# Casting and accumulating DMAs for part of the split of streamed weights, in a two-layer encoder trunk on one core

## The chip, the cores and the metric

One core of one Trainium2 chip runs the whole program in one launch. The metric is the device time of an execution in microseconds (us). Engines are called by the profile's names: PE multiplies matrices (PEld is its weight load), DVE, ACT and POOL work element by element, SP issues loads. A DMA is issued by an engine's instruction, runs by itself, and whoever needs its data waits for its landing.

## The reference

Two layers over 512 tokens of width 1024, all in float32: a feed-forward, a token mixer of three parallel attentions, and a second feed-forward; then a last norm.

```python
for l in range(DEPTH):                                   # 2
    x = x + 0.5 * swiglu(rms_norm(x, ffn1_norm[l]), ffn1_w13[l], ffn1_w2[l])   # 1024 -> 2 x 2816 -> 1024
    h = rms_norm(x, mix_norm[l])
    aq, ak, av, bq, bk, bv, cq, ckv, ckr = _split_cols(h @ w_in[l])
    oa, ob, oc = diff_attention(...), window_gqa(...), mla(...)
    proj = jnp.einsum('bsnw,nwd->bsnd', jnp.stack([oa, ob, oc], axis=2), w_branch[l])
    gates = jax.nn.sigmoid(h @ w_gate[l] + b_gate[l]).reshape(b, s_len, N_BRANCH, D_MODEL)
    x = x + jnp.sum(gates * proj, axis=2) @ w_out[l]
    x = x + 0.5 * swiglu(rms_norm(x, ffn2_norm[l]), ffn2_w13[l], ffn2_w2[l])
return rms_norm(x, final_norm)
```

## The kernel before

**Arithmetic.** Activations lie with features down the 128 partitions and the 512 tokens across. A float32 product is made of three products of the type fp32r: each factor is the sum of an upper part (the number rounded to fp32r) and a lower part (the rest), and `mm3` (lines 151 to 157) adds upper x upper (line 155), upper x lower (156) and lower x upper (157). Each is a product of 128x128 weights with 512 columns.

**The stream of weights.** All weights lie in DRAM in the order of their use, as 409 chunks of 128 x 1024 float32 (512 KB), eight blocks of 128x128 each. `Stream` (line 40) hands them out. `load` issues a chunk's load from SP into the tile `wraw` (3 buffers). `_split` (line 63) makes a chunk's parts: ACT copies `wraw` into `whi` (line 71; writing fp32r rounds), DVE subtracts, `wlo = wraw - whi` (line 72). `whi` and `wlo` have 3 buffers each (`WB`), so the parts of chunk c+3 can be written only when PE has done with chunk c. `take` (line 76) gives PE the next block; when it stands at the third block of chunk c, it calls for the split of chunk c+1. Chunk 0 is loaded and split in two pieces (`cuts`).

**Phases.** A feed-forward (`ffn`, line 361) uses 66 chunks: 44 for w13 (tiles `pa`, `pg`), 22 for w2 (tiles `po`). After each of the 8 output tiles of w2 DVE updates x (line 383), and POOL squares it and adds it to a running sum (`square_sum`, lines 254 to 261), for the next norm. The mixer (`mix`, line 740) lays projections (`acc`, `pm`, `pw`) between the steps of the attentions. In `rstd` (263) POOL's power (274) stands between two sets of transposes of PE.

**Order.** Each engine works through its own queue in order. In general the framework chooses the order within a queue by priority and by when it thinks that something is ready; so an instruction can stand ahead of others that were written before it. The start of the program is an exception: in the first feed-forward the order of ACT, DVE and POOL is that of the text, which asks for all eight square sums before the first `take`:

```python
with self.tc.manual_schedule(engines={nc.scalar.engine, nc.vector.engine, nc.gpsimd.engine}):
    for j in range(NT):
        self.next_h(j, None)          # square_sum on POOL
    _, R = self.group_rstd(pss, srcs, h, (6, 8))
```

`group_rstd` takes 48 blocks, which calls for the splits of chunks 0 to 6. Before it, PE multiplies zeros (line 296) eight times while the first loads are under way.

Of the kernel before, what the change touches and what calls it, by code (L numbers as in the profile page):

```python
# [18 lines left out]
T = 512  # L19
# [20 lines left out]
class Stream:  # L40
    """The weights, 128 rows by 128 columns at a time, in the order of their use."""

# [20 lines left out]
    def _split(self, upto):  # L63
        while self.ready < min(upto, self.k.nch):
            c = self.ready
            self.load(c + self.k.AHEAD)
            r = self.raw.pop(c)
            lo = self.k.wp.tile([P, CH], F32R, tag="wlo", bufs=self.k.WB, name="wlo")
            hi = self.k.wp.tile([P, CH], F32R, tag="whi", bufs=self.k.WB, name="whi")
            for part in self.cuts(c):  # L70
                self.k.nc.scalar.copy(hi[:, part], r[:, part])  # L71
                self.k.nc.vector.tensor_tensor(lo[:, part], r[:, part], hi[:, part].bitcast(F32), ALU.subtract)  # L72
            self.split[c] = (hi, lo)
            self.ready += 1
# [12 lines left out]
    def fit(self, width):  # L87
        """Fills a chunk that has no room for so wide a block."""
        while self.pos % CH + width > CH:
            self.order.append((None, P))  # L90
            self.pos += P


class Kernel:
    RAW, AHEAD, WB = 3, 2, 3  # chunks of weights: buffers as loaded, loads ahead, buffers of their parts
    UNITS, PTS = 72, 4  # tiles of 512 and of 1024 columns
    WARM = 8  # products of zeros that raise TensorE's clock while the first loads are under way
    LAG = 1  # steps between the scores of a block of queries and the rest
    FILL0, RATES = (0, 1), (0.35, 0.6, 0.85)  # how much other work goes between an attention's steps

# [11 lines left out]

    # ---- tiles
    def u(self, dt=F32, shape=(P, T), name="u"):
# [26 lines left out]

    # ---- pieces
    def lookup(self, *args, **kw):
        """An activation that needs a table of its own; these keep their order, so that tables change seldom."""
        if self.last is None:
            self.last = self.nc.scalar.activation(*args, **kw)
        else:
            with self.tc.issue_after(self.last.ins):
                self.last = self.nc.scalar.activation(*args, **kw)

    def mm3(self, ps, w, x, start, stop):
        """ps += w^T x, each float32 as the sum of two parts that one pass carries."""
        (wh, wl), (xh, xl) = w, x
        mm = self.nc.tensor.matmul
        mm(ps, wh, xh, start=start, stop=False)  # L155
        mm(ps, wh, xl, start=False, stop=False)  # L156
        mm(ps, wl, xh, start=False, stop=stop)  # L157

    def proj(self, ps, src, xs):
        """128 output features for all tokens; src(k) names a block of weights."""  # L160
        n = len(xs)
        for k in range(n):
            self.mm3(ps, self.w.take(src(k)), xs[k], k == 0, k == n - 1)
# [15 lines left out]
    def group(self, pss, srcs, xs):  # L179
        """Several projections side by side, so that the last of xs is needed late. With no xs,  # L180
        they are made on the way from x."""
        n = len(xs) or NT
        for k in range(n):
            for ps, src in zip(pss, srcs):
                while len(xs) < min(k + (1 if ps is pss[0] else 3), n):
                    xs.append(self.gsplit(self.x[len(xs)], self.g(0, G_FFN1, len(xs)), "h"))
                self.mm3(ps, self.w.take(src(k)), xs[k], k == 0, k == n - 1)
            yield

    def group_rstd(self, pss, srcs, xs, at=(4, 6)):  # L190
        """A group, with the scale of the tokens worked out meanwhile."""
        res = g = None
        for k, _ in enumerate(self.group(pss, srcs, xs), 1):
            if k in at:
                g = g or self.rstd(self.sqacc, D, self.att)
                try:
                    next(g)
                except StopIteration as e:
                    res = e.value
        return res  # L200
# [4 lines left out]
    def stacked(self, src, name):  # L205
        """The parts of two heads' rows, each head's one above the other: the first head's with the
        upper part on top, the second's with the lower one."""
        out = []
        for m in range(2):
            t = self.u(F32R, name=name)  # L210
            own, other = slice(m * 64, m * 64 + 64), slice(64 - m * 64, 128 - m * 64)
            self.nc.scalar.copy(t[own], src[own])
            self.nc.vector.tensor_tensor(t[other], src[own], t[own].bitcast(F32), ALU.subtract)
            out.append(t)
        return out

    def doubled(self, src, name):
        """Of two heads' rows, each head's upper part twice above each other, and the lower parts."""
        out = []
# [12 lines left out]
    def mm_stacked(self, ps, q, m, c, kh, kl, start, stop):  # L232
        """ps += q^T k over 64 rows: q as stacked, the upper part of k twice above each other."""
        own = slice(m * 64, m * 64 + 64)
        self.nc.tensor.matmul(ps, q[:, c], kh, start=start, stop=False)
        self.nc.tensor.matmul(ps, q[own, c], kl[own], start=False, stop=stop)
# [10 lines left out]
    def gsplit(self, src, g, name="g"):  # L247
        """The parts of src times a gain per partition."""
        hi, lo = self.pair(name)
        self.nc.scalar.activation(hi, src, AF.Copy, scale=g)  # L250
        self.nc.vector.scalar_tensor_tensor(lo, src, g, hi.bitcast(F32), ALU.mult, ALU.subtract)  # L251
        return hi, lo
# [10 lines left out]
    def rstd(self, acc, dim, bank, evac=True):  # L263
        """From sums of squares: 1/rms per token, down the partitions and across them. Yields
        where TensorE would wait."""
        nc = self.nc
# [17 lines left out]

    # ---- set-up
    def setup(self):
# [48 lines left out]

    # ---- feed-forward
    def next_h(self, j, gcol):
        """x's tile j is final: its part of the next norm's input."""
        h = None if gcol is None else self.gsplit(self.x[j], gcol, "h")
# [71 lines left out]

    # ---- the three mixers
    def scaled(self, ps, R, by=None):
# [7 lines left out]
    def rproj(self, src, xs, R, by=None):  # L421
        """A projection of normalised tokens: the scale of a token comes after the product."""
        ps = self.acc()
# [6 lines left out]
    def vproj(self, xs, src, out, banks):  # L430
        """Values with tokens down the partitions, 512 features wide."""
        pss = [b("pv") for b in banks]
# [25 lines left out]
    def flip(self, p, n, hi, lo):  # L458
        """The parts of p's transposed blocks; hi and lo take n blocks side by side."""
        ps = self.att("tp")  # L460
# [4 lines left out]
    def pv(self, ps, v, pth, ptl):  # L465
        """ps += values^T probabilities^T over four blocks of keys, for two blocks of queries."""
        mm = self.nc.tensor.matmul
# [7 lines left out]
    def full_pv(self, hd, qb, d, v, st):  # L475
        """Transposes the probabilities of a block of queries; after two blocks, their products with the values."""
        if qb == 0:
# [12 lines left out]
    def heads(self, n, steps, prepare, first, second):  # L490
        """All heads' steps in one line: scores of a step, then the rest of the step before; the
        next head's projections in between. Yields where other work may go."""
        todo = []
# [81 lines left out]
    def vproj_b(self, l, h, R, v):  # L575
        """Values of both key heads, each head's parts side by side."""
        t = yield from self.win(l, [(2176, P)], h, R)
# [16 lines left out]
    def branch_b(self, l, v, kk, h, R, qs, out):  # L594
# [42 lines left out]
        def second(j, hf, ps):  # L637
# [5 lines left out]
            for m in range(2):  # L643
# [6 lines left out]
                yield  # L650
                # above, the upper parts of the values; below, the lower ones
                side = slice(m * 256, m * 256 + 256)
# [87 lines left out]
    def mix(self, l):  # L740
# [26 lines left out]
        z2, z0, z1 = [], [], []  # L767
        # compressed projections of C
        cols = [[(2688 + i * P, P)] for i in range(2)] + [[(2944, 64), (2976, 32), (2944, 32)]] + [[(2304 + i * P, P)] for i in range(3)]
# [103 lines left out]
def gather(order, nch, inp):  # L873
    """The weights' blocks, in the order of their use."""
    out = np.zeros((P, nch * CH), np.float32)
    at = 0
# [85 lines left out]
```

## Time and profile before

| | us |
|---|---|
| median of 2 runs (2548.07 to 2548.37) | 2548.22 |
| span of the profiled execution | 2544.7 |
| PE busy in it | 2524.1 |
| DVE busy | 1355.1 |
| ACT busy | 936.2 |
| POOL busy | 270.6 |

The span runs from the first to the last instruction of the profiled execution; the runs are 3.5 us above it. A product's row shows 0.39 us, but products are pipelined: the next one starts 0.23 us later, and that is the pace. A row of the timeline gives start, duration, engine, line, operation, what it writes and reads, and in square brackets how long the engine was idle before it and what ended that.

### The profile page before, as it was taken

To read this page: it belongs to the slowest core of one execution; us is meant where nothing else is said; L and a number is where in the kernel's file an instruction comes from. 1 tells how busy PE (TensorE), PEld (TensorE's weight loads), DVE (VectorE), ACT (ScalarE), POOL (GpSimd) and SP (SyncE) were. 2 spreads that over 40 slices of the span, in tenths; PEclk is the share of its full clock that TensorE was granted. 3 is DMA by queue.
4 is the path that set the end of the run, shared out by engine and by line. 5 is a ranking of instruction groups with operands and counts; after the bars stand their busy time and mean duration, and the time that the engine had idled before them with its cause. 6 is when DMAs were issued, how large, how long until landed. Compare 5 with 4: busy or idle time off the path is not lost.

```text
span 2544.7 us, 28509 instructions
## 1 busy us (share of the span) xinstructions
PE 2524.1 (99%) x11424; PEld 2044.0 (80%) x11424; DVE 1355.1 (53%) x2004; ACT 936.2 (37%) x1429; POOL 270.6 (11%) x208
## 2 busy tenths in 40 slices
PE   9999999999999999999999999999999999999997
PEld 7888887777777888888888888877777788888886
DVE  6444336666667554443344443366666676544433
ACT  4332223365555433332233322244655553322211
POOL 4000123000001220001100001130000014100011
PEclk9999999999999999999999999999999999999999
DMA  4333332112212233333333333321222122333331
GB/s 159 93 97 100 95 122 86 59 58 75 67 58 67 88 94 100 93 97 100 95 96 100 93 98 99 106 81 51 67 75 66 56 70 89 102 97 94 100 99 67
DMA packets 62484, 223.22 MB, mean 88 GB/s; under 512 B 7200, under 2 KB 7344, under 8 KB 62352
## 3 DMA queue, kind: packets, MB, share of 16 engines
q1 hardware_dynamic: 60912, 217.67, 27.6%
q0 software_dynamic: 864, 2.70, 0.3%
q8 instruction: 89, 1.46, 0.2%
q10 hardware_dynamic: 576, 1.05, 0.1%
q14 instruction: 43, 0.35, 0.0%
HBM read 219.29 MB, written 2.10 MB: 87 GB/s over the span
## 4 chain that ended last, share of the span: by engine, by line
PE 95%; DVE 3%; ACT 1%; issue 1%; POOL 0%; DMA 0%; SPq 0%; DVEq 0%; POOLq 0%; ACTq 0%
PE pa L157 7%; PE pa L155 7%; PE pa L156 7%; PE acc L155 7%; PE po L155 6%; PE po L157 6%; PE po L156 6%; PE acc L156 6%; PE acc L157 6%; PE pg L156 5%; PE pg L155 5%; PE pg L157 5%; PE tp L462 2%; PE pm L155 2%; PE pm L157 2%; PE pm L156 2%
## 5 line engine op out<-in xcount | busy, mean ns | idle before, releaser
L72 DVE TENSOR_TENSOR wlo<-wraw,whi 128x1024 fp32r<-128x1024 f32 (+1 forms) x410 | 526.8, 1285 | 641.9 <-ACT whi L71 640.7
L71 ACT CAST whi<-wraw 128x1024 fp32r<-128x1024 f32 (+1 forms) x410 | 429.7, 1049 | 820.0 <-PE po L156 254.4
L155 PE MATMUL pa<-hh,whi 128*128 128x512 f32 x800 | 312.6, 391 | 0.9 <-DVE x L851 0.9
L157 PE MATMUL pa<-hh,wlo 128*128 128x512 f32 x800 | 311.7, 390 | 1.0 <-DVE wlo L72 1.0
L156 PE MATMUL pa<-hl,whi 128*128 128x512 f32 x800 | 311.7, 390 | 0.0
L155 PE MATMUL acc<-hh,whi 128*128 128x512 f32 x672 | 275.4, 410 | 0.0
L156 PE MATMUL acc<-hl,whi 128*128 128x512 f32 x672 | 263.9, 393 | 0.0
L157 PE MATMUL acc<-hh,wlo 128*128 128x512 f32 x672 | 263.5, 392 | 0.0
L155 PE MATMUL pg<-hh,whi 128*128 128x512 f32 x608 | 236.5, 389 | 0.0
L156 PE MATMUL pg<-hl,whi 128*128 128x512 f32 x608 | 236.5, 389 | 0.0
L157 PE MATMUL pg<-hh,wlo 128*128 128x512 f32 x608 | 236.5, 389 | 0.0
L155 PE MATMUL po<-ah,whi 128*128 128x512 f32 x576 | 224.1, 389 | 0.0
L156 PE MATMUL po<-al,whi 128*128 128x512 f32 x576 | 224.1, 389 | 0.0
L157 PE MATMUL po<-ah,wlo 128*128 128x512 f32 x576 | 224.1, 389 | 0.0
L155 PEld LDWEIGHTS pa<-hh,whi 128*128 128x128 f32 x800 | 150.4, 188 | 33.2 <-DVE x L851 1.3
L157 PEld LDWEIGHTS pa<-hh,wlo 128*128 128x128 f32 x800 | 150.3, 188 | 33.1 <-DVE wlo L72 1.9
L156 PEld LDWEIGHTS pa<-hl,whi 128*128 128x128 f32 x800 | 150.3, 188 | 31.2 <-DVE hl L251 0.3
L155 PEld LDWEIGHTS acc<-hh,whi 128*128 128x128 f32 x672 | 126.3, 188 | 32.5 <-issue 9.0
L157 PEld LDWEIGHTS acc<-hh,wlo 128*128 128x128 f32 x672 | 126.2, 188 | 27.7 <-issue 0.2
L156 PEld LDWEIGHTS acc<-hl,whi 128*128 128x128 f32 x672 | 126.6, 188 | 22.3 <-issue 0.9
L155 PEld LDWEIGHTS pg<-hh,whi 128*128 128x128 f32 x608 | 114.2, 188 | 23.8
L157 PEld LDWEIGHTS pg<-hh,wlo 128*128 128x128 f32 x608 | 114.1, 188 | 23.7
(248 smaller groups left out, 3906.5 us busy)
## 6 DMA issues: line engine op xcount, KB each, us to landing
wraw<-in_w SPq DMA_DIRECT2D x408, 512.0 KB, 3.5
x<-in_x SPq DMA_DIRECT2D x8, 256.0 KB, 6.4
rope<-in_rope POOLq DMA_DIRECT2D x6, 256.0 KB, 3.7
out<-o ACTq DMA_DIRECT2D x4, 256.0 KB, 2.9
out<-o SPq DMA_DIRECT2D x4, 256.0 KB, 3.4
dist<-in_cst POOLq DMA_DIRECT2D x1, 448.0 KB, 4.0
wraw<-in_w SPq DMA_DIRECT2D x1, 384.0 KB, 4.6
lv<-in_lam POOLq DMA_DIRECT2D x1, 256.0 KB, 3.9
```

The costliest lines, as they stand in the source:

```text
L71: self.k.nc.scalar.copy(hi[:, part], r[:, part])
L72: self.k.nc.vector.tensor_tensor(lo[:, part], r[:, part], hi[:, part].bitcast(F32), ALU.subtract)
L155: mm(ps, wh, xh, start=start, stop=False)
L156: mm(ps, wh, xl, start=False, stop=False)
L157: mm(ps, wl, xh, start=False, stop=stop)
L462: self.nc.tensor.transpose(ps[:, i * P:(i + 1) * P], p[:, i * P:(i + 1) * P], self.ident)
```

## The change

Of four chunks (counted c % 4) two are split in another way; loads, buffers and order of the rest stay as written.

- c % 4 == 1: `whi` isn't copied by ACT. POOL issues a DMA from DRAM that reads the chunk a second time and converts it to fp32r. DVE still subtracts.
- c % 4 == 3: ACT copies `whi` as before. Then ACT writes `wlo = -wraw` (rounded to fp32r), and POOL issues a DMA that adds `wraw` to `wlo`. DVE doesn't subtract.

```diff
             hi = self.k.wp.tile([P, CH], F32R, tag="whi", bufs=self.k.WB, name="whi")
+            nc = self.k.nc
             for part in self.cuts(c):
-                self.k.nc.scalar.copy(hi[:, part], r[:, part])
-                self.k.nc.vector.tensor_tensor(lo[:, part], r[:, part], hi[:, part].bitcast(F32), ALU.subtract)
+                if c % 4 == 1:
+                    nc.gpsimd.dma_start(hi[:, part], self.k.ws[c][:, part])
+                else:
+                    nc.scalar.copy(hi[:, part], r[:, part])
+                if c % 4 == 3:
+                    nc.scalar.mul(lo[:, part], r[:, part], -1.0)
+                    nc.gpsimd.dma_start(lo[:, part], r[:, part], accum_op=ALU.add)
+                else:
+                    nc.vector.tensor_tensor(lo[:, part], r[:, part], hi[:, part].bitcast(F32), ALU.subtract)
```

Besides, comments and docstrings are gone.

## Rows read from the trace of the kernel before

**Rows 1.** The page: busy time of the engines; PE's granted clock in 40 slices.
```profile
PE 2524.1 (99%) x11424; PEld 2044.0 (80%) x11424; DVE 1355.1 (53%) x2004; ACT 936.2 (37%) x1429; POOL 270.6 (11%) x208
PEclk9999999999999999999999999999999999999999
```

**Rows 2.** Waits of PE: for whom, us in total, times, longest.
```profile
PE pr L278 <- POOL r L274: 3.6, 3, 2.1
PE st L269 <- DVE sqacc L392: 2.2, 1, 2.2
PE pa L157 <- DVE wlo L72: 1.0, 2, 0.7
```

**Rows 3.** The page's groups: the two instructions of the split.
```profile
L72 DVE TENSOR_TENSOR wlo<-wraw,whi 128x1024 fp32r<-128x1024 f32 (+1 forms) x410 | 526.8, 1285 | 641.9 <-ACT whi L71 640.7
L71 ACT CAST whi<-wraw 128x1024 fp32r<-128x1024 f32 (+1 forms) x410 | 429.7, 1049 | 820.0 <-PE po L156 254.4
```

**Rows 4.** Timeline in w13 of the first feed-forward: a split, its first user.
```profile
101.44 1.05 ACT L71 CAST whi<-wraw 128x1024 fp32r<-128x1024 f32 x1 [3.11 <-PE pa L156]
102.53 1.23 DVE L72 TENSOR_TENSOR wlo<-wraw,whi 128x1024 fp32r<-128x1024 f32 x1 [0.21 <-ACT whi L71]
112.30 0.39 PE L155 MATMUL pg<-hh,whi 128*128 128x512 f32 x1
112.32 1.05 ACT L71 CAST whi<-wraw 128x1024 fp32r<-128x1024 f32 x1 [3.11 <-PE pa L156]
112.76 0.39 PE L157 MATMUL pg<-hh,wlo 128*128 128x512 f32 x1
```

**Rows 5.** DMA queue of the weights, and issues: KB each, us to landing.
```profile
q1 hardware_dynamic: 60912, 217.67, 27.6%
wraw<-in_w SPq DMA_DIRECT2D x408, 512.0 KB, 3.5
rope<-in_rope POOLq DMA_DIRECT2D x6, 256.0 KB, 3.7
dist<-in_cst POOLq DMA_DIRECT2D x1, 448.0 KB, 4.0
DMA to landing us min/median/max: 3.1/3.5/7.2
```

**Rows 6.** Timeline of POOL at the start.
```profile
9.56 1.62 POOL L261 TENSOR_TENSOR sqacc<-sqacc,sq 128x512 f32<-128x512 f32 x1
11.15 1.49 POOL L260 TENSOR_TENSOR sq<-x 128x512 f32<-128x512 f32 x1
...
31.11 1.28 POOL L261 TENSOR_TENSOR sqacc<-sqacc,sq 128x512 f32<-128x512 f32 x1
```

**Rows 7.** Timeline of DVE and PE at the start.
```profile
11.66 2.06 DVE L72 TENSOR_TENSOR wlo<-wraw,whi 128x1024 fp32r<-128x1024 f32 x1
1.49 3.78 PE L296 MATMUL idle<-idle 128*128 128x512 f32 x8 [1.49 <-DVE idle L293]
12.42 0.39 PE L155 MATMUL pa<-hh,whi 128*128 128x512 f32 x1
13.77 0.50 PE L157 MATMUL pa<-hh,wlo 128*128 128x512 f32 x1 [0.74 <-DVE wlo L72]
```

**Rows 8.** POOL's square sums: durations in ns, min/median/max.
```profile
L260 POOL TENSOR_TENSOR sq<-x x48: 1039/1042/2023, 7.8 to 2515.0; 128x512 f32<-128x512 f32 x48
L261 POOL TENSOR_TENSOR sqacc<-sqacc,sq x48: 1282/1618/2155, 9.6 to 2516.2; 128x512 f32<-128x512 f32 x48
```

**Rows 9.** Stretches: us, busy time by engine, PEclk, DMA share, GB/s.
```profile
560.00:850.00 290.00, 289.56 (x1376) 226.33 (x1376) 193.44 (x404) 155.30 (x306) 20.77 (x18) 1.00 0.22 69
2530.00:2544.00 14.00, 1.77 (x8) 1.13 (x8) 5.63 (x10) 1.10 (x2) 3.52 (x3) 0.59 0.40 150
```

**Rows 10.** Timeline in the mixer: the split that comes latest, its user.
```profile
551.52 1.99 ACT L71 CAST whi<-wraw 128x1024 fp32r<-128x1024 f32 x2
561.18 0.39 PE L155 MATMUL acc<-hh,whi 128*128 128x512 f32 x1
```

## The prediction, made before the changed kernel ran

> **What bounds the kernel now.** I read the page first: PE is busy for 99% of the span and its clock is granted in full throughout [rows 1]. Next, the waits of PE: the three largest are 3.6, 2.2 and 1.0 us in the whole run, and only the last is for weights [rows 2]. So time is the number of products times 0.23 us, and no relief of another engine can give back more than about 10 us. The change can only leave PE fed, or starve it. What decides is how early a chunk's parts are ready.
>
> That is read from the timeline in w13 [rows 4]. A chunk there feeds PE for 24 products, 5.44 us. ACT's copy at 101.44 waited for PE's last product with the buffer's old content, and starts as soon as that ends. Two more chunks lie in between: the next copy, at 112.32, starts with PE's first product of the next chunk but one, and the first user of the chunk copied at 101.44 is the product at 112.30; its lower part is first read at 112.76. From the release of the buffer a chunk has thus 10.9 us to get its upper part, 11.3 us to get the lower one. Copy and subtraction use 2.3 us of it (102.53 + 1.23 = 103.76). So 8 to 9 us are spare, chunk after chunk. Four feed-forwards of 66 chunks go like this, 264 of 409. In the mixer a chunk takes longer, as attention's products lie between: 72 chunks in some 540 us, 7.5 us each.
>
> **What the change removes.** Chunks 0 to 408 hold 102 of each changed kind. DVE loses 102 subtractions of 1.285 us [rows 3], 131 us. ACT loses 102 copies and gains 102 negations of the same size, both about 1.05 us [rows 3]: nothing. Neither engine sets the end [rows 2], so I cost the relief at 0; what hides it is PE's own queue of products.
>
> **The casting DMA in the steady stages.** No DMA of before converts. POOL's plain loads land 3.7 us (256 KB) and 4.0 us (448 KB) after their issue [rows 5]; by that slope 512 KB take 4.1 us. The weights' own loads from SP land in 3.5 us, at most 7.2 us [rows 5]. Lower bound 3.5, upper 7.2; I take 4.1, the row of the same queue. With DVE's subtraction behind it (1.29 us) the lower part is there 5.4 us after the release, at most 8.5 us, of 11.3: hidden. DVE's queue stands at that subtraction until the DMA lands, some 3 us longer than it stood for ACT, and evacuations of PSUM stand behind it. In w13 the next of those is due one chunk (5.44 us) later; in the mixer DVE is busy for 193 of 290 us [rows 9] and softmax steps stand behind it, with PE having projections to do meanwhile. I put 4 us on this for the whole run, an estimate between 0 and the 10 us that all waits of PE amount to now.
>
> **The accumulating DMA in the steady stages.** It waits for copy and negation: 2 x 1.05 = 2.1 us. Then it reads `wraw` and the old `wlo` and writes `wlo`. The queue of the weights shows what a plain 512 KB cost in transfer: 27.6% of 2544.7 us for 217.67 MB [rows 5], that is 702 us for 415 pieces, 1.7 us each. Lower bound of the landing 3.5 us, as a plain load; with a second reading 4.1 + 1.7 = 5.8 us, which I take, being an estimate from the nearest rows; upper 7.2 + 1.7 = 8.9 us. The lower part is ready at 2.1 + 5.8 = 7.9 us, at most 11.0 us, of 11.3. Hidden, but by 0.3 us only at the far end. PE would begin to wait when the DMA needs more than 11.3 - 2.1 = 9.2 us. The tightest place in the mixer is chunk 91 (91 % 4 = 3, counted along line 71): the second of the two copies at 551.52 ends at 553.5, and its first user is the product at 561.18 [rows 10]; 553.5 + 1.05 + 5.8 = 560.4, just in time.
>
> `wraw` is held longer, until the DMA has read it, so the load of chunk c+3 is issued about 8 us after the release instead of 2.3. It lands by about 12, and is wanted by a copy 16.3 us (three chunks) after the release: hidden. The DMA engines go from 28% to at most 28 + 7 (casting) + 14 (accumulating, twice) = 49%.
>
> **The start.** Here POOL's queue decides. The order is written by hand: eight square sums, then the splits. Chunk 1 is the first with c % 4 == 1, so its upper part, made by ACT at 9.71 before, now comes from a DMA that POOL can issue only behind all square sums, which end at 31.11 + 1.28 = 32.4 us [rows 6]. PE wants that part at 12.42 [rows 7]. All other blocks add to the same sums behind it; PE stands.
>
> How long? DVE stops at its subtraction of chunk 1 (before at 11.66 [rows 7]), waiting for the same DMA, and no longer slows POOL: a pair of square and sum goes from up to 2.02 + 2.16 down to 1.04 + 1.28 us [rows 8], 2.44 us with the gaps. Six pairs are left at 11.15 [rows 6]: they end at 11.15 + 14.6 = 25.8 us. DMA 4.1 us: 29.9. Subtraction 1.29 us and a tenth: 31.3. The product that read this lower part at 13.77 [rows 7] so comes 17.5 us later. Bounds: 25.8 + 3.5 + 1.3 - 13.8 = 16.8 us below; 32.4 + 7.2 + 2.1 - 13.8 = 27.9 us above. I take 17.5, since DVE certainly stops. By the Trainium skill (DMA: Bandwidth & Descriptors, section "Anatomy of one DMA"), a DMA issued from GpSimd takes 2.0 us plus its bytes at 436 GB/s, an estimate of 3.2 us for 512 KB; the rows say 4.1, and by the page this term would be 16.6.
>
> PE idles some 17 us in this. The profile shows what that does to its clock: behind the last products, in 2530 to 2544 with PE busy for 1.8 us, the granted clock is 0.59 [rows 9], and at the start the first eight products (of zeros) took 3.78 us, 0.47 each instead of 0.23 [rows 7]. If eight to ten products go at half pace after the stall, that is 2 us. Range 0 to 3.
>
> Chunk 3's accumulation stands behind chunk 1's DMA on POOL, but is issued at about 27 us for a need beyond 42; chunk 5's cast waits for chunk 2's buffer. Both are hidden by PE's own delay. POOL's power for the first norm comes behind them and is not wanted before block 48.
>
> **Sum.** 17.5 + 2 + 4 = 23.5 us. The profiled execution's 2544.7 becomes 2568; the runs lie 3.5 us above it, 2548.2 becomes about 2572.
>
> **Rivals.**
> (1) The accumulating DMA is slow. From 9.2 us on, each of the 66 of the feed-forwards costs PE the excess: at 11 us 66 x 1.8 = 119 us, hence 2690; the whole passes 2% (51 us, what a measurement of this kernel can tell from no change) at 9.2 + 27.5 / 66 = 9.6 us. Against it: the upper bound by rows is 8.9. For it: nothing in the trace accumulates. What would push it over is a mechanism like this: POOL's writing of a DMA's orders waits out instructions of DVE; one subtraction of 1.29 us before each would make it 5.8 + 1.3 = 7.1, two 8.4, three 9.7. The Trainium skill (SBUF — State Buffer, sections "SBUF: two separate sides" and "Who interferes with whom") has that rule for DVE's two-port modes and not for two-input instructions like this subtraction; by it, an estimate, the steady chunks of w13 lose nothing. No row of before shows such a DMA under DVE's load. Chance 0.14.
> (2) POOL's order in the steady stages. A DMA can stand behind a square sum that itself waits for x. If the framework leaves DMAs where they are written, at a chunk's third block, 6 blocks or 4.1 us ahead of need, a cast lands 4.1 + 1.3 us later, and behind a square sum some 3 us later still. Of 22 chunks of w2 11 are changed; if 4 in each of four feed-forwards stand so, 16 x 3 = 48 us: 2620. Against it: ACT's copies are written at the same place and yet go at the release [rows 4], so such instructions are moved ahead. Chance 0.06.
> (3) The start costs nothing, because the DMA of chunk 1, which waits for nothing, is put ahead of the square sums despite the order by hand: 2548 + 4 = 2552. ACT and DVE keep the text's order there, so I give it 0.09.
> (4) Faster by 2%: only if DVE, 131 us lighter, was what held PE. Waits of PE of 10 us in all exclude it: 0.01.
>
> **How the numbers follow.** Forecast as summed, 0.70, its own range 2560 to 2590 (start from 16.8 to 27.9, clock 0 to 3, steady 0 to 10): 2572. Rivals (3) 0.09, (2) 0.06, (1) 0.14. The range for 8 in 10 takes in the forecast and part of (3) and (2): 2552 to 2620. Slower by over 2% (above 2599): (1), (2) and a rest, 0.20. Faster 0.01. Within 2%: 0.79.
>
> **What would show it.** In the changed profile: PE idle from about 13 to 31 us, its waits naming `whi` or `wlo` of chunk 1, and POOL's first casting DMA right behind the last sum at about 26 us. In w13, landings of accumulations under 9 us, and no waits of PE for `wlo`. DVE's busy time down by 131 us, ACT's unchanged. Wrong I am if PE's waits name `wlo` in every fourth chunk (rival 1), if they gather in w2 (rival 2), or if PE is busy at 20 us (rival 3).

## The result, and the profile after

The changed kernel takes 2579.16 us (2577.81 and 2580.52) against 2548.22: 1.0121 times as long, 95% interval 1.0102 to 1.0141. That is 31 us more. The forecast was 2572 in a range of 2552 to 2620. The profiled execution has a span of 2576.0 us, 31.3 above that of before.

The page of the changed kernel, engines, granted clock, POOL's DMA queue and the two new kinds of DMA (KB each, us to landing):

```profile
PE 2528.4 (98%) x11424; PEld 2043.9 (79%) x11424; DVE 1230.2 (48%) x1902; ACT 930.1 (36%) x1429; POOL 408.1 (16%) x412
...
PEclk8999999999999999999999999999999999999998
...
q1 hardware_dynamic: 60912, 217.67, 26.3%
q0 software_dynamic: 30240, 109.67, 18.5%
...
whi<-in_w POOLq DMA_DIRECT2D x102, 512.0 KB, 3.9
wlo<-wraw POOLq DMA_DIRECT2D x102, 512.0 KB, 4.6
```

DVE is 125 us lighter than in [rows 1], ACT 6 us. PE has the same 11424 products and is busy for only 4 us more: what is lost is idle PE. The waits of PE (us in total, times, longest) against [rows 2]:

```profile
PE pa L163 <- DMA whi<-in_w: 17.2, 1, 17.2
PE pr L286 <- POOL r L282: 6.1, 6, 2.1
PE st L277 <- DVE sqacc L400: 2.2, 1, 2.2
PE cs L710 <- ACT kch L248: 2.1, 2, 1.3
PE acc L163 <- DVE vl L259: 2.0, 1, 2.0
PE po L480 <- DVE ptl L249: 2.0, 2, 1.5
```

One wait of 17.2 us names a casting DMA. The rest is small and scattered, and names POOL, DVE and ACT, not the new DMAs. Lines have moved: 163 to 165 are `mm3` (before 155 to 157), 73 the casting DMA, 75 ACT's copy, 77 its negation, 78 the accumulating DMA, 80 DVE's subtraction, 282 POOL's power.

**Where the 31.3 us are.** The n-th product of PE after, set beside the n-th before, tells how far PE is behind. The order of products differs only inside the mixers (345 of 11424 have other names), so the shift is read at the borders of stages. Each row is one profiled execution against the one of before.

| kernel (below) | shift at 60 us | behind mixer 1 | behind mixer 2 | span |
|---|---|---|---|---|
| changed | 19.2 | 23.2 | 28.8 | +31.3 |
| start as before | 1.7 | 5.9 | 13.2 | +15.9 |
| chunk 1's cast first | 15.2 | 19.3 | 27.2 | +30.1 |
| feed-forwards only | 1.8 | 1.3 | 1.3 | +1.3 |
| chunk 1 only | 19.2 | 19.3 | 19.2 | +19.4 |
| mixers only | 0.4 | 3.8 | 10.0 | +10.9 |
| mixers, casts only | 1.7 | 7.0 | 13.0 | +13.1 |
| mixers, accumulations only | 1.4 | 0.4 | 0.6 | +0.6 |
| mixers, copy after | 1.8 | 1.8 | 1.9 | +2.4 |
| without the costly places | 1.9 | 0.3 | 0.5 | +0.5 |

In the four kernels of the table whose names begin with "mixers" the start is that of before, and still it comes out 0.4 to 1.8 us later. The execution of before that was profiled is one of the shorter ones: its span is 2544.7 us, and other executions of the same kernel have 2543.9 to 2547.6. So shifts under 2 us at the start say nothing. For the changed kernel the table reads: start 19, first mixer 4.1, second mixer 5.6, the four feed-forwards 0 to a tenth, and 2.5 us behind the last product. By medians of several executions the start alone costs 17 to 18 us (runs "chunk 1 only" and "start as before").

**The start**, timelines of POOL, DVE and PE of the changed kernel:

```profile
24.26 1.26 POOL L269 TENSOR_TENSOR sqacc<-sqacc,sq 128x512 f32<-128x512 f32 x1
25.46 0.58 POOL L73 DMA_DIRECT2D whi<-in_w  x1
26.04 0.93 POOL L78 DMA_DIRECT2D wlo<-wraw  x1
...
29.58 1.22 DVE L80 TENSOR_TENSOR wlo<-wraw,whi 128x1024 fp32r<-128x1024 f32 x1 [18.00 <-DMA whi<-in_w]
...
29.60 0.79 PE L163 MATMUL pa<-hh,whi 128*128 128x512 f32 x1 [17.18 <-DMA whi<-in_w]
```

The casting DMA is issued right behind the last square sum, at 25.46 us; before, that sum ended at 32.4 with DVE at work beside it [rows 6]. PE, which had its product at 12.42 [rows 7], has it at 29.60. Its first twelve products then go at a slower pace, one every 0.43 to 0.67 us instead of 0.23, and the shift grows from 17.2 to 19.1 us. In the 5.6 us from 29.60 on, which they fill, the granted clock is 0.50, the lower of its two levels, 1.2 of 2.4 GHz; from 35.3 on it is 1.00. The stretch from 30 to 60 us (columns as in [rows 9]) has a granted clock of 0.91 where it was 1.00 before:

```profile
30.00:60.00 30.00, 29.96 (x123) 24.03 (x123) 9.72 (x12) 4.74 (x5) 3.45 (x3) 0.91 0.48 142
```

**The steady stages.** A stretch of 140 us in w13 of the first feed-forward:

```profile
95.00:235.00 140.00, 140.00 (x619) 115.95 (x618) 55.42 (x70) 42.48 (x53) 9.39 (x13) 1.00 0.52 145
```

The landings of the casting DMAs, then of the accumulating ones, over the whole run:

```profile
DMA to landing us min/median/max: 3.7/3.9/5.6
...
DMA to landing us min/median/max: 4.5/4.6/6.0
```

PE is busy for all of it. A casting DMA needs at most 5.6 us, with a subtraction of 1.3 us behind it, and the lower part had 11.3 us [rows 4]. An accumulating one needs at most 6.0 us, and there was room for 9.2.

**The second mixer**, DVE and PE of the changed kernel:

```profile
1709.31 1.66 DVE L80 TENSOR_TENSOR wlo<-wraw,whi 128x1024 fp32r<-128x1024 f32 x1 [5.23 <-DMA whi<-in_w]
1710.89 2.71 DVE L259 SCALAR_TENSOR_TENSOR vl<-pv,r,vh 128x512 fp32r<-128x512 f32 x4
...
1711.68 0.50 PE L163 MATMUL acc<-hh,whi 128*128 128x512 f32 x1 [2.03 <-DVE vl L259]
```

DVE stands for 5.23 us at a subtraction whose upper part hasn't landed. Behind it in DVE's queue are four instructions that empty PSUM tiles, and PE waits 2.03 us for one of them. The chunk itself isn't wanted yet. From 1702 to 1713 us PE's shift grows from 23.2 to 26.6: 3.4 of the 5.6 us of this mixer. Beside the 2.03 us PE waits 0.9 and 1.4 us there for POOL's two powers; before, its waits for POOL came to 1.1 us in the whole mixer.

That the part comes so late has a reason in POOL's queue. ACT's copy of this chunk (281) and POOL's first power, in the kernel before:

```profile
1677.20 1.05 ACT L71 CAST whi<-wraw 128x1024 fp32r<-128x1024 f32 x1 [2.73 <-issue]
1679.28 1.02 POOL L274 TENSOR_TENSOR r<-ms,mhalf 128x4 f32<-128x4 f32 x1 [3.77 <-DVE ms L272]
```

POOL's power and the casting DMA, in the changed kernel:

```profile
1703.35 1.03 POOL L282 TENSOR_TENSOR r<-ms,mhalf 128x4 f32<-128x4 f32 x1 [3.64 <-DVE ms L280]
1704.72 0.63 POOL L73 DMA_DIRECT2D whi<-in_w  x1 [0.34 <-issue]
```

PE was 23.2 us behind then, so ACT's copy would have stood at 1700.4, and the buffer was free by that time. The DMA is issued 4.3 us later, because it stands behind a power that waits 3.64 us for DVE. Issued at 1700.4 it would have held DVE for about 1 us instead of 5.23, an estimate from the 4.6 us to its landing. Of the 36 casts of the mixers 31 are issued at most 1 us later than ACT's copies of before, moved by PE's shift; of the other five this one is the latest.

### The profile page after: what moved, and what is told of

Read it like the earlier page. It is cut to its first block, busy times and chain, and to the rows that moved or that the text cites. A ratio compares the mean times of both kernels' runs of the same rounds, so it can differ in the third digit from the quotient of the medians.

```text
span 2576.0 us, 28842 instructions
## 1 busy us (share of the span) xinstructions
PE 2528.4 (98%) x11424; PEld 2043.9 (79%) x11424; DVE 1230.2 (48%) x1902; ACT 930.1 (36%) x1429; POOL 408.1 (16%) x412
## 5 line engine op out<-in xcount | busy, mean ns | idle before, releaser
L80 DVE TENSOR_TENSOR wlo<-wraw,whi 128x1024 fp32r<-128x1024 f32 (+1 forms) x308 | 391.4, 1273 | 577.0 <-ACT whi L75 301.4
L75 ACT CAST whi<-wraw 128x1024 fp32r<-128x1024 f32 (+1 forms) x308 | 322.5, 1047 | 701.5 <-PE po L164 270.2
L163 PE MATMUL pa<-hh,whi 128*128 128x512 f32 x800 | 313.5, 392 | 18.1 <-DMA whi<-in_w 17.2
L78 POOL DMA_DIRECT2D wlo<-wraw x102 | 90.3, 885 | 1023.3 <-ACT wlo L77 665.3
L73 POOL DMA_DIRECT2D whi<-in_w x102 | 57.8, 567 | 684.6 <-PE pa L165 177.0
```

The costliest lines, as they stand in the source:

```text
L73: nc.gpsimd.dma_start(hi[:, part], self.k.ws[c][:, part])
L78: nc.gpsimd.dma_start(lo[:, part], r[:, part], accum_op=ALU.add)
```

## The experiments

All times but one (accumulate three times) are medians of several executions beside several of the kernel before; the ratios are to those. Where the trace tells more finely than the times, the table above is quoted.

**Start as before.** Chunks 1 and 3 split as in the kernel before.

```diff
-                if c % 4 == 1:
+                if c % 4 == 1 and c > 4:
-                if c % 4 == 3:
+                if c % 4 == 3 and c > 4:
```

> Chunks 1 and 3 are split as in the kernel before, all other chunks as in the changed one. Theory (the start's stall is additive): the changed kernel's first 60 us lose 19.1 us (17.2 of PE's wait for chunk 1's upper part, 1.9 of slow products after it). They go, but chunk 5's casting DMA now is the first behind the square sums: they end at about 32.4, it lands at 36.5, DVE's lower part is there at 37.7, and PE wants it at 36.1: 1.6 us. 2579.2 - 19.1 + 1.6 = 2561.7; range 2559 to 2564. Rival (the DMAs' general load costs PE time wherever it runs, the start is only where it shows first): the rest of the run takes up part of what the start gives back, 2568 or more.

Measured: 2560.96 us, 1.0052 (1.0037 to 1.0067). 18 us of the 31 are gone, and the rest of the run doesn't take them up. The mixers cost 4.2 and 7.4 us here. The 1.6 us for chunk 5 can't be told from the spread of the start, and no wait of PE there names a casting DMA.

**Chunk 1's cast first.** The casting DMA of chunk 1 is written ahead of the square sums, nothing else moves. (Not shown: the split of chunk 1 takes this tile and issues no DMA of its own.)

```diff
+                self.w.first = self.wp.tile([P, CH], F32R, tag="whi", bufs=self.WB, name="whi")
+                nc.gpsimd.dma_start(self.w.first, self.ws[1])
                 for j in range(NT):
                     self.next_h(j, None)
```

> As the changed kernel, but the casting DMA of chunk 1 is written ahead of the eight square sums. Theory (the place in POOL's queue is what costs): PE no longer waits for chunk 1, but chunk 3's accumulating DMA is still behind the square sums. Those end at about 32.5 with DVE at work beside them; 0.9 + 4.6 us later it has landed, 37.5, and PE wants the lower part at 24.8: a new stall of 12.7 us, and about 1 of slow products. 2548.2 + 13.7 + 9.7 (mixers) + 2.5 (end) = 2574; range 2571 to 2578. Rival A (chunk 1's DMA is late by itself, whatever its place): stays at 2579. Rival B (only the cast counts, the accumulation is hidden): 2560.

Measured: 2576.1 us, 1.0111 (1.0096 to 1.0126). PE's longest wait:

```profile
PE pa L166 <- DMA wlo<-wraw: 11.0, 1, 11.0
```

The stall for chunk 1 is gone and chunk 3's accumulation, still behind the sums, has taken its place: shift at 60 us 15.2 instead of 19.2. Rivals A and B fall. It is the place in POOL's queue that costs: chunk 1's DMA behind the sums, and with that one out of the way chunk 3's. A DMA for which PE has more time there, as chunk 5's in the run above, costs nothing that can be told from the spread.

**Chunk 1 only.**

```diff
-                if c % 4 == 1:
+                if c == 1:
-                if c % 4 == 3:
+                if False:
```

> Only chunk 1 gets its upper part by a casting DMA, everything else is as in the kernel before. Theory: the whole start's loss with nothing else, 2548.2 + 19.1 = 2567.3, and no longer closing drain, as POOL's queue held one DMA more only; range 2566 to 2569. Rival (the stall is shared with chunk 3's accumulation, or the lateness is caught up later because ACT and DVE get ahead during it): under 2562.

Measured: 2564.89 us, 1.0069 (1.0054 to 1.0084), 17 us more than before and 1 us under the range expected. One DMA of 409 chunks makes more than half of the whole loss. The shift is 19.2 at 60 us and 19.2 at the end: PE catches nothing up, since it had no idle time to catch up with.

**Feed-forwards only.** Both conditions get `and c > 4 and not (66 <= c < 138 or 270 <= c < 342)`.

> DMAs only for chunks of the feed-forwards from chunk 5 on; chunks 1 and 3 and those of both mixers (66 to 137, 270 to 341) are split as before. Theory (hidden in the feed-forwards, all remaining cost sits in the mixers and at the end): 2548.2 + 1.6 (chunk 5) + 2.5 (closing drain of POOL) = 2552.3; range 2549 to 2554. Rival (66 casts and 66 accumulations of the feed-forwards cost a tenth each): 2562 or more.

Measured: 2547.69 us, 1.000 (0.9991 to 1.001). 65 casts and 65 accumulations (those of the feed-forwards less chunks 1 and 3) cost nothing. The 2.5 us expected at the end didn't come either.

**Mixers only**, the complement: both conditions get `and (66 <= c < 138 or 270 <= c < 342)`.

> DMAs only for the chunks of the two mixers (66 to 137, 270 to 341), everything else split as in the kernel before: the complement of the run with feed-forwards only. Theory: all that the changed kernel loses beside its start sits here, 11.5 us by the run with the start as before (4.1 and 7.4 us in the two mixers), and up to 2.5 us in POOL's closing drain: 2547.7 + 11.5 = 2559.2, with the drain 2561.7; range 2556 to 2562. Rival (the loss needs DMAs in the feed-forwards as well, whose traffic makes the mixers' loads late): under 2553.

Measured: 2558.65 us, 1.004 (1.0025 to 1.0055): 10 us, with a shift of 3.3 and 6.2 us over the two mixers. The loss needs no DMAs elsewhere.

**Mixers, casts only; mixers, accumulations only.** Of the two conditions of the kernel above one is made `False`.

> Only the casting DMAs, only in the mixers. Theory A (DVE stands at its subtraction until the cast has landed, with evacuations behind it that PE waits for, and POOL's power stands behind the DMA's issue): most of the 11.5 us, 7 or more: 2555 to 2560. Theory B (the accumulations carry the loss, by the longer issue of 0.9 us on POOL and the later landing): 3 us or less, under 2551.

> Only the accumulating DMAs, only in the mixers. Theory A: nothing on DVE waits for them, only POOL's queue is longer: 4 us or less, 2548 to 2552. Theory B (the accumulations carry the loss): 7 us or more, 2555 to 2560.

Measured: casts 2559.44 us, 1.0043 (1.0026 to 1.006); accumulations 2547.39 us, 0.9996 (0.9987 to 1.0005). The casts carry all of it. 36 accumulations, with the longer issue (0.88 us against 0.56) and the later landing, cost nothing. Theory B falls. DVE's wait for casts in the kernel with casts only, and in its timeline the place that answers to the one shown above:

```profile
DVE wlo L80 <- DMA whi<-in_w: 46.0, 19, 8.1
```

```profile
1693.31 1.23 DVE L80 TENSOR_TENSOR wlo<-wraw,whi 128x1024 fp32r<-128x1024 f32 x1 [4.35 <-DMA whi<-in_w]
1694.45 2.72 DVE L259 SCALAR_TENSOR_TENSOR vl<-pv,r,vh 128x512 fp32r<-128x512 f32 x4
```

**Mixers, idle cast (inconclusive).** To take DVE's wait away and keep POOL's queue, ACT copies as before and the cast goes into a tile that nobody reads. There are no accumulations here or in the next run (those lines of the edit are left out).

```diff
+                if c % 4 == 1 and (66 <= c < 138 or 270 <= c < 342):
+                    nc.gpsimd.dma_start(self.k.scratch, self.k.ws[c][:, 0:512])
```

> As the run with casts in the mixers only, but each casting DMA there writes a tile that nobody reads (the first 512 of the chunk's 1024 columns, so half the bytes), and ACT copies the upper part as in the kernel before. DVE waits for no DMA; POOL's queue holds the same issues. Theory (two causes side by side: DVE standing at its subtraction until the landing, and POOL's power or square sums standing behind a DMA's issue that waits): only the second is left, by PE's waits for POOL some 4 us: 2550 to 2555. Rival A (POOL's queue is all of it): 2558 or more. Rival B (DVE's standing is all of it): 2549 or less.

Measured: 2585.01 us, 1.0145 (1.0128 to 1.0161). Nothing in the program read what these DMAs wrote, and the framework moved all 36 to the front: they run from 2 to 139 us, ahead of and between the square sums. The shift is 38 us at 60 us and doesn't grow afterwards. It says nothing of the mixers, and once more that the start is where POOL's queue costs PE.

**Mixers, copy after.** The same with a tie: the DMA reads the upper part that ACT has just made, so it can't leave its place.

```diff
             self.split[c] = (hi, lo)
+            if c % 4 == 1 and (66 <= c < 138 or 270 <= c < 342):
+                nc.gpsimd.dma_start(self.k.scratch, hi[:, 0:512].bitcast(F32))
```

> Casts in the mixers only, in number and place on POOL as in the run with casts there, but each is issued after ACT has made the upper part as in the kernel before, reads that (half of its columns) and writes a tile that nobody reads. So DVE waits for no DMA, while POOL's queue keeps the issues at nearly the same places among its other work. Theory (two causes: DVE standing at its subtraction until a cast has landed; POOL's powers and sums standing behind a DMA's issue): the second alone is left, by PE's waits for POOL in the run with casts (5.7 us in the mixers against 1.4 before) some 4 us: 2550 to 2555. Rival A (POOL's queue is all of it): 2558 or more. Rival B (DVE's standing is all of it, directly or by what queues behind it): 2549 or less.

Measured: 2548.08 us, 1.000 (0.9991 to 1.001). No loss. POOL's queue at the place that cost most, with the DMA between the two powers just as in the kernel with casts:

```profile
1681.12 1.04 POOL L284 TENSOR_TENSOR r<-ms,mhalf 128x4 f32<-128x4 f32 x1 [3.77 <-DVE ms L282]
1682.13 0.62 POOL L82 DMA_DIRECT2D scratch<-whi  x1
1682.93 1.03 POOL L284 TENSOR_TENSOR r<-ms,mhalf 128x4 f32<-128x4 f32 x1 [0.18 <-DVE ms L282]
```

The theory of two causes falls, rival B stands: what stands behind the new DMAs in POOL's queue costs nothing in the mixers. PE's waits for POOL's power go back to the 3.6 us of [rows 2], though the DMA still stands between the two powers; so in the kernel with casts they depend on DVE's being late. What the kernel with casts has and this one hasn't is DVE waiting for a DMA. (Its DMAs also read DRAM, twice the bytes, and land later, 3.9 us against 2.3. No wait of PE there names a cast, and the weights' loads land in 3.6 us in both, so that this reaches PE by another way is not seen; no run excludes it by itself.)

One thing this run can't show: what the casts themselves lose by what stands in front of them on POOL. Nobody reads its DMAs, so their being late holds up no one. For chunk 281 the timelines above show that loss, 4.3 us, and in the kernel with casts the same place looks alike (issue at 1689.25, behind a power at 1688.24 that waited 3.76 us for DVE). A run that issues this one cast ahead of the power was not made.

**Accumulate three times.** Each accumulation from chunk 5 on is followed by two more that add zeros; the sum is unchanged.

```diff
                     nc.gpsimd.dma_start(lo[:, part], r[:, part], accum_op=ALU.add)
+                    if c > 4:
+                        for _ in range(2):
+                            nc.gpsimd.dma_start(lo.rearrange("p (a b) -> p a b", a=2), self.k.zero[:, None, :].broadcast_to([P, 2, 512]), accum_op=ALU.add)
```

> As the changed kernel, but from chunk 5 on each accumulation is followed by two more into the same tile that add zeros, each waiting for the one before. Theory (a chunk's lower part has 11.3 us from the release of its buffer, and 9.2 us of that for DMAs): 2.1 + 3 x 4.7 = 16.2 us, so PE waits 4.9 us for the lower part of every fourth chunk of the feed-forwards, 65 times, 319 us, and a part of the mixers' 36 as well: 2579 + 320 + 0 to 60, 2890 to 2960. Its waits name the lower part. Rival (there is more room than that, because the framework's order gives the chunk a longer lead when the DMA is known to be long): under 2700.

Measured: 3626.54 us, one execution. Far more than expected, and the reason is in the added DMAs, not in the room. One chunk, ACT's copy and negation, POOL's three DMAs, PE's first product with the lower part (timeline):

```profile
155.94 1.05 ACT L75 CAST whi<-wraw 128x1024 fp32r<-128x1024 f32 x1 [1.98 <-PE pa L167]
...
158.24 0.86 POOL L78 DMA_DIRECT2D wlo<-wraw  x1 [17.42 <-ACT wlo L77]
163.01 1.19 POOL L81 DMA_DIRECT2D wlo<-zero  x1 [3.92 <-DMA wlo<-wraw]
171.00 1.19 POOL L81 DMA_DIRECT2D wlo<-zero  x1 [6.79 <-DMA wlo<-zero]
...
177.06 0.77 PE L168 MATMUL pg<-hh,wlo 128*128 128x512 f32 x1 [8.51 <-DMA wlo<-zero]
```

Of PE's waits in that kernel the longest in total:

```profile
PE pa L168 <- DMA wlo<-zero: 313.8, 33, 10.5
```

The real accumulation takes 4.8 us, the zeros (two rows of 2 KB a partition, from one) 8.0 and 6.0. The lower part is there 21.1 us after the copy's start; the room is 11.3; PE should wait 9.8 us. It waits 8.5: its first product with the chunk's upper part comes at 166.80, 10.9 us after the copy's start as in [rows 4], and five products of `pa`, 1.1 us, stand in PE's queue before the one that waits. So the room read off [rows 4] is right, and my price for the added DMAs, 4.7 us each, was wrong. The waits also lower the clock: it is 1.00 in the 12.6 us ahead of this wait and 0.50 in the 5 us behind it, and 0.870 in the mean of this execution.

**Without the costly places.** The changed kernel with chunks 1 and 3 and the mixers' casts taken back; 65 casts and 101 accumulations stay.

```diff
-                if c % 4 == 1:
+                if c % 4 == 1 and c > 4 and not (66 <= c < 138 or 270 <= c < 342):
-                if c % 4 == 3:
+                if c % 4 == 3 and c > 4:
```

> The changed kernel without the casts that were found costly: chunks 1 and 3 and the casts of both mixers are split as before; 66 casts in the feed-forwards and 101 accumulations stay. Theory: chunk 5's cast at the start 1.8 us, all else hidden: 2548 to 2551. Rival (cast and accumulation cost something together that neither does alone): 2555 or more.

Measured: 2546.99 us, 0.9996 (0.9987 to 1.0005). The same as before. 166 of the 204 DMAs can stay at no cost, and bring nothing: PE's waits are again of the size of those in [rows 2]. No run points to a version that beats the kernel before.

## Why the prediction was right, and where it was short

**The bound.** PE's queue sets the end. Held: DVE gave back 125 us and the time got longer by 31; without the costly places the two kernels are equal. The sum was 23.5 us, and 31 were measured: the forecast of 2572 is 7 us short, inside its range. The two terms below make up the difference, 5.6 us in the mixers and 2.5 at the end; the start and the feed-forwards were right to half a microsecond.

**The start.** Predicted: sums end at 25.8, stall 17.5, slow products 2. Measured: 25.46 (the DMA's issue), 17.2, 1.9. That DVE would halt, and so speed up POOL's sums, was what brought the end of the sums down from 32.4 to 25.8: a pair of square and sum took 2.33 us from 13.79 on, put at 2.44. That chunk 3's accumulation is hidden by PE's own delay held as well, and the run with chunk 1's cast first shows what it costs when that cover is gone: PE's wait of 11.0 us. The landing was put at 4.1 us, by rows, and this one DMA took that (issued at 25.46, DVE went on at 29.58); the casting DMAs have 3.7 at least and 3.9 in the median, so 0.2 us of that fit is luck. The estimate of 3.2 us by the Trainium skill (DMA: Bandwidth & Descriptors, "Anatomy of one DMA") is 0.7 us under that median.

**The steady stages of the feed-forwards.** Predicted: hidden. Held, to a tenth of a microsecond. The accumulating DMA was put at 5.8 us between 3.5 and 8.9; it is 4.6. Rival 1 needed 9.2. The rule of the Trainium skill (SBUF — State Buffer, "SBUF: two separate sides") on DMAs starved by DVE names DVE's two-port modes and not a two-input subtraction. The trace agrees as far as it goes: with DVE busy for 40% of that stretch the longest landing of a new DMA in the run is 6.0 us. Rival 2 (order in w2) fell too: PE lost nothing there. What it describes, a DMA behind an instruction of POOL that itself waits, is what happened to chunk 281 in the mixer. Rival 3, the cast put ahead of the sums by the framework, didn't come. But in the idle cast DMAs were moved ahead of the sums: those lay outside the part whose order is by hand.

**The mixers: the term that was mis-sized.** I put 4 us on DVE's queue standing at the subtraction, "an estimate between 0 and the 10 us that all waits of PE amount to now". It measured 9.6 us in the changed kernel and up to 11.5 in the variants. The mechanism was the one named: DVE stands at its subtraction, other work stands behind it, PE waits. The size came from no row of the mixer's own chain. I looked at how long a chunk has until PE wants it, and there is plenty, where I should have looked at what stands behind the subtraction in DVE's queue and how soon PE wants that. In the second mixer it is the four evacuations of the value projection, which PE waits for 2.0 us; together with POOL's powers that place makes 3.4 of the 9.6 us. The rest is in waits of 1.5 us and less, seen one by one in no experiment. The prediction also let every cast be issued when its buffer is free; at that place it stood 4.3 us behind POOL's power, which waited for DVE for 3.77 us already in the kernel before.

**The end: a term that was missing.** Behind the last product the changed kernel loses 2.5 us more. The closing instructions of POOL (line 953; durations in ns, min/median/max) in the changed kernel:

```profile
L953 POOLq DRAIN  x3: 51/244/10092, 2564.7 to 2575.7; - x3
```

The longest drain takes 10.1 us, from 2564.7 to 2574.8, and the last output has landed at 2572.3; before it took 3.8 and was over before the last output had landed. I had left POOL's end out of the sum.

## What to carry to other kernels

A DMA put in place of an engine's instruction lands hidden when its consumer has room, and that room is read from the release of the buffer to the first use, not from the mean share of busy time. But it also takes a place in two queues: that of the engine that issues it, where it waits behind all that stands in front, and that of the engine that reads it, where all that stands behind must wait with it. Both larger losses here came from a queue: 17 to 19 us behind POOL's square sums at the start, 10 us in the mixers where DVE stood at a subtraction with other work behind it, a third of that at one place where the cast itself stood behind POOL's work. And where PE is busy for 99% of the span, a lost stretch is never caught up, nor is any relief of another engine worth anything.

## What the runs showed of the hardware

- A casting DMA of 512 KB from DRAM into fp32r lands in 3.9 us in the median, hardly behind a plain load from SP (3.6 in the same run); an accumulating one within SBUF in 4.6. POOL is occupied for 0.56 and 0.88 us by their issue.
- An accumulating DMA that reads one row of 2 KB a partition twice is slower: 6.0 us to landing in the median against 4.5 for the others in that kernel, 8.0 where I followed one through. POOL is occupied for 1.2 us by its issue. Why stays open.
- After 17 us without a product PE's clock is granted at 0.50 for 5.6 us, twelve products, and then at 1.00 again.
- POOL's closing drain was 3.8 us with up to 15 DMAs issued by POOL, 6.6 to 7.4 us with 50 to 180, and 9.9 to 10.1 us in the three kernels with 216 or 218, but 6.5 us in the one with 420. It delays the end only where it is the longest. What sets it stays open.
